# Two gate products behind the first scores of the attention phase, and both halves of a split weight taken into its plan

## The chip, the cores and the metric

The kernel runs on one core of one Trainium2 chip. The metric is the device time of one execution in microseconds; of several executions the median is taken. The core has five engines with instruction queues of their own: TensorE (PE in the profile, matrix products into PSUM), VectorE (DVE), ScalarE (ACT), GpSimd (POOL) and SyncE (SP, here for DMAs alone). An engine runs its queue in order and waits for others on semaphores.

## What is computed

One layer over 1024 tokens of width 1024 with 256 context tokens, in float32. Two attentions run side by side on one projection of the modulated input: A sees a window of 128 tokens to each side plus the context, B sees everything. Both are merged with sigmoid gates per channel, go through an output product, a residual and a layer norm, and then a feed-forward part with a short convolution. What the change touches is this part:

```python
proj = h @ w_in + b_in
o_a = _windowed_attention(q_a, k_a, v_a, k_a_c, v_a_c, sink.reshape(A_KV_HEADS, A_GROUPS))
o_b = _global_attention(q_b, jnp.concatenate([k_b, k_b_c], axis=1), jnp.concatenate([v_b, v_b_c], axis=1))
g_a, g_b = jnp.split(jax.nn.sigmoid(gate_logits), 2, axis=-1)
return (g_a * (o_a @ w_branch_a) + g_b * (o_b @ w_branch_b)) @ w_out
```

## The kernel before

Matrix products are made in three passes, since each float32 operand is split into a rounded high part and the rest as a low part: high x high, high x low, low x high (`mm3`, lines 345 to 347). Whoever makes such a pair casts the value (line 337 in `split`, or 1145) and subtracts the cast from it (342, or 1151). Much of the work of ACT, VectorE and POOL is this splitting.

The run has three phases. In the first, to 333.5 us, the input is modulated and projected. The steps stand in a fixed order (`GORD`), in which the 16 gate blocks of 128 channels fill in between the other projections; the last four stand at the end. `gate(f, hf)` makes one half of a block: 24 matmuls of 512 columns into a PSUM bank, a Sigmoid on ACT (line 920), and a store to the DRAM tensor `sgd`, issued from ACT's queue (921). Blocks 0 to 7 are A's gates, 8 to 15 are B's.

The second phase, 333.5 to 734 us, is the attention. It has 32 units: branch (16 units of A, then 16 of B), block i of 128 tokens, and key head g with its four query heads. A unit goes through these steps:

- scores of four heads on TensorE (`s` or `pt` banks, lines 720 and 721, with a mask, 743 or 745);
- per head the maximum and its negative on VectorE (`pm`, line 754), then the exponential on ACT (`ex`, line 763), which also sums. For A the sink logit stands in an extra column of the probabilities `pa`, which POOL writes once (line 1029);
- the reciprocal of the sums (782), which takes a way of its own over a transpose `pts` and DMAs;
- per tile of 128 keys four transposes on TensorE (808) into a `pt` bank, whose result is cast to a high part `hi` (ACT, 1145) and a low part `lo` (VectorE, 1151; for a few tiles POOL), and then two matmuls with V into the bank `av` (817);
- a copy of `av` by ACT (1165), then on POOL the steps `up`, `ot` (822), the multiplication by the reciprocal (1176), and the high and low part of the output tile `O` (834 and 831);
- two units ahead, the query is split, transposed (699), cast (704) and moved by DMAs (708, 709).

The order of this phase on all five engines is written by a list planner. `graph` makes one entry per step, with a cost of its engine from the table `COST`, a due time from the table `KEY`, what it follows and which buffers it takes (`RINGS`; the PSUM banks are three `pt`, two `s` of two banks, one `av`). `plan` then picks, engine by engine, the entry that is due first among those that can start within `SLACK` of the earliest, out of the next `LOOK`. The kernel is recorded in that order, so none of the constants acts at run time.

Into the plan go also the output product of A, and a part of B's. That product with `w_b` has eight channel blocks f, each in two token halves hf; a weight block holds two values of f. `group` (12 matmuls, 2.7 us) makes one half of one f, and VectorE multiplies by the gate (`gmul`, line 1064). Weight block 0 of B is split by POOL within the plan (hwb1_0, lwb1_0), and the first halves of f = 8 and 9 (the 0 and 1 of B) are made there. Blocks 1 and 2 are loaded at the end of the plan. After it, ACT casts and VectorE subtracts them, TensorE makes the first halves of f = 2 and 3 with block 1 (`half`), then the second halves of 0 and 1 (`rest`), which need the output of the last unit, and so on up to 7. `merge` adds A's and B's part and splits the sum. Then follow the product with `w_out` and the third phase, which the change leaves alone.

Of the kernel before, what the change touches and what calls it, by code (L numbers as in the profile page):

```python
# [13 lines left out]
P = 128  # L14
D = 1024
T = 1024
# [26 lines left out]
POOLED, FILL, SUMS = ((3,), (2, 6)), (16.57, 27.12), ('ot1', 'ot1')  # L43
LOOK, SLACK = 16, (0, 0, 0, 0.038, 0)
# [25 lines left out]
class Buf:  # L70
    def __init__(self, ring, slot=None):
        self.ring, self.fix, self.slot, self.left, self.end = ring, slot, None, 0, 0.0
# [13 lines left out]
def plan(ops, rings, free, look, slack):  # L86
# [5 lines left out]
    while any(todo):  # L92
# [25 lines left out]
        for b in o.uses:  # L118
# [20 lines left out]
    bm=(DVE, .61, .77), sd=(SP, .6, 9.0), sp=(POOL, 1.2, 10.0),  # L139
)  # L140
PORT = "nr1", "ot0", "ot1", "qlo", "pl", "tt", "ol", "wl"

RINGS = dict(pt=3, s=2, av=1, qs=1, q1=2, q2=2, p=8, hi=4, lo=4, ptr=2, up=1, ot=1, rb=2, wraw=1, wh=1, wl=1)

KEY = {'qh': -2.357, 'qt': -0.903, 'sc': 0.037, 'scs': (0.114, 0.286),
           'scx': -0.84, 'tr': 0.706, 'tru': (0.168, 0.1),
           'av': 1.325, 'st': 1.084, 'out': 1.875, 'exd': 0.896, 'st1': 1.52, 'wb': 29.511, 'wg': 32.061}
# [3 lines left out]
def graph(x, key=KEY, pooled=((3,), (2, 6)), fill=None, ot=("ot0", "ot1")):  # L151
# [12 lines left out]
    avs_of = {}  # L164
    units = []
    for u in range(UNITS):
# [36 lines left out]
        for h in range(4):  # L203
# [6 lines left out]
            o = op(f"sc{br}", k, lambda u=u, h=h, s=s: x.sc(u, h, s), [qr], [s], [q1, q2])  # L210
            if nar:
                o.occ, o.lat = o.occ - .11, o.lat - .11
            chain("sc", o)
            m = op(f"pm{br}", k, lambda u=u, h=h, s=s, p=p[h]: x.pm(u, h, s, p), [o, other[h] if br else None],
                   [p[h]], [s])
            chain("pm", m)
            e = op(f"ex{br}", k + key["exd"], lambda u=u, h=h: x.ex(u, h), [m], uses=[p[h]])
# [79 lines left out]
    raw = Buf("wraw")  # L297
    k = key["wb"]
    a = op("ld", k, lambda r=raw: x.ld(4, r), [units[27]["qlo"], grps[-1]], [raw])
    b_ = op("wh", k + .1, lambda r=raw: x.wh(4, r, None), [a], uses=[raw])  # L300
    c = op("wl", k + .1, lambda r=raw: x.wl(4, r, None), [b_], uses=[raw])
    for n in (0, 1):
        pt = Buf("pt")
        d = op("sg", UNITS - 1 + .1 * n, lambda f=8 + n: x.sg(f, 0), end)
        e = op("grp", key["wg"] + .3 * n, lambda f=8 + n, p=pt: x.grp(f, 0, p), [b_, c] + [units[u]["ol"] for u in range(16, 24)], [pt])
        op("bm", UNITS - .5 + .1 * n, lambda f=8 + n, p=pt: x.bm(f, 0, p), [e, d], uses=[pt])
        op("ld", UNITS - .8 + .1 * n, lambda f=1 + n: x.rw(f), end)
# [15 lines left out]
def layer_kernel(  # L323
# [348 lines left out]
    class Unit:  # L672
# [57 lines left out]
        def scores(self, h, s):  # L730
            kh = self.br * 2 + self.g
            if h == 0 and not self.br:
                self.begin()
# [1399 lines left out]
```

## Time and profile before

| | us |
|---|---|
| median of three runs | 1532.3 (1531.63 to 1532.4) |
| the profiled execution | 1530.37 |
| its span, first to last instruction | 1528.6 |
| TensorE busy | 1512.9 |
| VectorE, ACT, POOL busy | 1144.8, 802.1, 773.5 |

The profiled execution lies 1.9 us below the median, and 1.8 us of it lie around the span. The clock that TensorE was granted is full throughout. In the rows of the profile, a name left of `<-` is the tile that is written, those right of it are read; a bracket at the end gives the idle time of the engine just before the instruction and what released it. A matmul's duration is modelled and reaches over the start of the next one, so that the distance between starts tells more of TensorE's pace than the durations do.

### The profile page before, as it was taken

Reading aid. Unit: us, or ns where it says so; the run is one execution under the profiler, and the core shown is the slowest. Engines: PE = TensorE matmul, PEld = TensorE weight load, DVE = VectorE, ACT = ScalarE, POOL = GpSimd, SP = SyncE. Lnnn points to the kernel's source line nnn. Section 1 sums busy time; section 2 is a strip of 40 time slices with the busy share of each in tenths; the row PEclk is TensorE's granted clock in tenths of the full one; section 3 lists DMA queues with packets and bytes.
Section 4 is the critical chain, followed back from the end, with each engine's and each line's share of the span. In section 5 each row is a group of like instructions: output and inputs, shape, how many; then the busy total and the mean of one; then the engine's idle time right before and its main releaser. Section 6 shows DMA issues by size and latency. Waiting matters only on the chain. (4 is left out here: it accounts for less than half of the span.)

```text
span 1528.6 us, 21924 instructions
## 1 busy us (share of the span) xinstructions
PE 1512.9 (99%) x7652; PEld 1269.9 (83%) x7652; DVE 1144.8 (75%) x1719; ACT 802.1 (52%) x1404; POOL 773.5 (51%) x737
## 2 busy tenths in 40 slices
PE   9999999999999999999999999999999999999997
PEld 7888888888988888888788988888888888888886
DVE  7488847627776777787665878888888887656797
ACT  5422223449887777798332574444444444435543
POOL 0365303418887565574333556666676674021063
PEclk9999999999999999999999999999999999999999
DMA  9667663312256663742460222333334446996723
GB/s 379 236 234 254 213 239 110 100 49 56 57 151 157 176 149 79 169 95 68 169 173 35 97 86 108 112 110 112 112 102 111 110 111 177 373 281 207 253 91 111
DMA packets 111873, 229.73 MB, mean 150 GB/s; under 512 B 13489, under 2 KB 27313, under 8 KB 111666
## 3 DMA queue, kind: packets, MB, share of 16 engines
q1 hardware_dynamic: 96464, 199.20, 39.0%
q0 software_dynamic: 10400, 20.19, 8.4%
q10 hardware_dynamic: 4898, 8.94, 1.6%
q8 instruction: 60, 0.98, 0.3%
q14 instruction: 51, 0.42, 0.1%
HBM read 177.09 MB, written 65.87 MB: 159 GB/s over the span
## 5 line engine op out<-in xcount | busy, mean ns | idle before, releaser
L1151 DVE TENSOR_TENSOR lo<-pt,hi 128x512 fp32r<-128x512 f32 x188 | 126.4, 688 | 42.8 <-ACT hi L1145 41.3
L342 DVE TENSOR_TENSOR ld<-rd,hd 128x1024 fp32r<-128x1024 f32 x77 | 97.8, 1287 | 49.6 <-ACT hd L337 47.4
L1145 ACT CAST hi<-pt 128x512 fp32r<-128x512 f32 x188 | 109.6, 584 | 47.3 <-PE pt L808 39.1
L337 ACT CAST hd<-rd 128x1024 fp32r<-128x1024 f32 x77 | 79.4, 1050 | 85.8 <-PE p L347 55.7
L345 PE MATMUL p<-hd 128*128 128x512 f32 x264 | 103.2, 391 | 0.0
L346 PE MATMUL p<-ld,hd 128*128 128x512 f32 x264 | 102.8, 389 | 0.2 <-DVE ld L342 0.2
L347 PE MATMUL p<-hd,ld 128*128 128x512 f32 x264 | 102.8, 389 | 0.0
L817 PE MATMUL av<-lo,VT 128*128 128x512 f32 x236 | 101.5, 435 | 0.2 <-POOL lo L1151 0.2
L817 PE MATMUL av<-hi,VT 128*128 128x512 f32 x236 | 100.5, 433 | 0.0
L347 PE MATMUL g<-hh,wlg 128*128 128x512 f32 x256 | 99.7, 390 | 0.4 <-POOL wlg L342 0.4
L345 PE MATMUL g<-hh,whg 128*128 128x512 f32 x256 | 99.9, 390 | 0.0
L346 PE MATMUL g<-hl,whg 128*128 128x512 f32 x256 | 99.6, 389 | 0.0
L754 DVE TENSOR_SCALAR_CACHE_REDUCE p<-s,cvt,nmc 128x1024 f32<-128x1024 f32 x64 | 85.8, 1340 | 16.4 <-PE s L721 9.3
L342 POOL TENSOR_TENSOR wlg<-wg,whg 128x512 fp32r<-128x512 f32 x32 | 45.3, 1423 | 99.3 <-ACT whg L337 93.7
L763 ACT ACTIVATE p<-p,nm 128x1024 f32<-128x1024 f32 x64 | 74.0, 1157 | 13.0 <-DVE p L754 12.4
L808 PE MATMUL pt<-ident,p 128*128 128x128 f32 x512 | 76.8, 272 | 0.0
L808 PEld LDWEIGHTS pt<-ident,p 128*128 128x128 f32 x512 | 62.7, 140 | 15.4 <-DVE lo L1151 0.2
L337 ACT CAST wS<-s 128x512 fp32r<-128x512 f32 x76 | 45.3, 620 | 52.1 <-POOL s L1465 51.3
L720 PE MATMUL s<-KL,q 128*128 128x512 f32 (+2 forms) x184 | 72.4, 393 | 0.0
L721 PE MATMUL s<-KL,q 128*128 128x512 f32 (+2 forms) x184 | 69.0, 375 | 0.2 <-DMA q<-q 0.2
L337 ACT CAST wA<-ru 128x512 fp32r<-128x512 f32 x57 | 35.5, 623 | 59.6 <-PE d L347 31.8
L342 DVE TENSOR_TENSOR wS<-s,wS 128x512 fp32r<-128x512 f32 x57 | 55.5, 1000 | 11.1 <-ACT wS L337 11.1
(432 smaller groups left out, 5019.2 us busy)
## 6 DMA issues: line engine op xcount, KB each, us to landing
wml<-in_wmodT_dram SPq DMA_DIRECT2D x48, 512.0 KB
ru<-in_w_up_dram SPq DMA_DIRECT2D x38, 512.0 KB
rd<-td SPq DMA_DIRECT2D x55, 256.0 KB
rd<-sd SPq DMA_DIRECT2D x44, 256.0 KB
rd<-in_w_dn_dram SPq DMA_DIRECT2D x33, 256.0 KB
wm<-in_wmodT_dram SPq DMA_DIRECT2D x16, 512.0 KB
wg<-in_w_g_dram SPq DMA_DIRECT2D x32, 256.0 KB
sgd<-sg ACTq DMA_DIRECT2D x32, 256.0 KB
```

What stands on the lines that cost most here:

```text
L337: cast[:] = [nc.scalar.copy(hi, src).ins]
L342: low[:] = [lo_eng.tensor_tensor(out=lo, in0=src, in1=hi.bitcast(F32), op=ALU.subtract).ins]
L345: nc.tensor.matmul(ps, a[0], b[0], start=start, stop=False, skip_group_check=resumed)
L346: nc.tensor.matmul(ps, a[0], b[1], start=False, stop=False, skip_group_check=resumed)
L347: return nc.tensor.matmul(ps, a[1], b[0], start=False, stop=stop, skip_group_check=resumed).ins
L720: nc.tensor.matmul(o, self.q1[:, hs], ks, start=True, stop=False)
L754: nc.vector.tensor_scalar(out=p if self.br else p[:, self.pad + 1:SINK + 1], in0=self.sv[h], scalar1=self.scale()[:, hs] if self.br else - ...
L763: nc.scalar.activation(o, i, AF.Exp, bias=self.nm[:, hs], scale=-1.0, accum_out=acc)
L808: nc.tensor.transpose(tr[:, h * P:(h + 1) * P], src, ident)
L817: nc.tensor.matmul(self.av, v, self.parts[n][low], start=first, stop=self.left == 0)
L1145: nc.scalar.copy(hi, units[u].parts[n])
L1151: e.tensor_tensor(out=lo, in0=src, in1=hi.bitcast(F32), op=ALU.subtract)
```

## The change

It has three parts.

1. The two halves of gate block 15 are left out of the projection loop. Behind it come first the scores of unit 0, all four heads, into the banks of `pt0`, `pt1`, `s0` and `s1`; then the 48 matmuls of gate 15 into the banks of `pt2` and `av0`; then the plan. The sigmoid of this block is made as 1 / (1 + exp(-x)): Exp on ACT (`ge`), plus one on POOL (`ga`), eight reciprocals of 128 x 128 on VectorE (`gr`), and two stores from SP (`gd`), all of them planned. The sink columns of `pa` are written in two portions of four, the second one planned.
2. Blocks 0 and 1 of `w_b` are both split by POOL within the plan, into spare output tiles, and the first halves of all four f = 0 to 3 are made there. Only block 2 is loaded at the end of the plan and split behind it. After the plan come the second halves of f = 0 to 3 (`rest`), each followed by its merge, then f = 4 to 7 with both halves (`both`).
3. `KEY`, `FILL`, `LOOK` and `SLACK` have new values, and narrow units count as cheaper, so that the plan orders the whole phase anew.

```diff
-POOLED, FILL, SUMS = ((3,), (2, 6)), (16.57, 27.12), ('ot1', 'ot1')
-LOOK, SLACK = 16, (0, 0, 0, 0.038, 0)
+POOLED, FILL, SUMS = ((3,), (2, 6)), (16.13, 25.4), ('ot1', 'ot1')
+LOOK, SLACK = 24, (0, 0, 0, 0.11, 0.209)
...
+    for hf in (0, 1):
+        b = Buf("pt", 2) if hf == 0 else Buf("av", 0)
+        gates.append(op("gate", -90.0 + hf, None, gates[-1:], [b]))
+        e = op("ge", key["ge"], lambda hf=hf, r=tile: x.ge(hf, r), [gates[-1]], [tile] if hf == 0 else [], [b] + [tile] * hf)
...
+        e = op("ga", key["ge"], lambda hf=hf: x.ga(hf), [e], uses=[tile])
+        for c in range(4):
+            r = op("gr", key["gr"] + .6 * (4 * hf + c), lambda hf=hf, c=c: x.gr(hf, c), [e], uses=[tile])
+        op("gd", key["gr"] + .6 * (4 * hf + c), lambda hf=hf: x.gd(hf), [r], uses=[tile])
...
+            if k == 2 * KT - 1:
+                continue
             gate(k, a)
...
+    for h, tag in enumerate(("pt0_", "pt1_", "s0_", "s1_")):
+        units[0].scores(h, ps2.tile([P, 512 * (1 + h // 2)], F32, tag=tag, name=f"s0_{h}", bufs=1))
+    gps = [ps2.tile([P, 512], F32, tag=tag, name="g15", bufs=1) for tag in ("pt2_", "av0_")]
+    for hf in (0, 1):
+        for k in range(KT):
+            w = [t[:, k % 4 * P:(k % 4 + 1) * P] for t in ready["g", 2 * KT - 1, k // 4]]
+            mm3(gps[hf], w, [t[:, hsl(hf)] for t in hT[k]], k == 0, k == KT - 1)
...
+        def ge(self, hf, r):
+            if hf == 0:
+                self.gt = at(r, "g").rearrange("p (a b) c -> p a (b c)", a=2)
+            nc.scalar.activation(self.gt[:, hf], gps[hf], AF.Exp, bias=bmc[:, 8:9], scale=-1.0)
+
+        def ga(self, hf):
+            nc.gpsimd.tensor_scalar(out=self.gt[:, hf], in0=self.gt[:, hf], scalar1=1.0, scalar2=1.0, op0=ALU.mult,
+                                    op1=ALU.add)
+
+        def gr(self, hf, c):
+            t = self.gt[:, hf, c * P:(c + 1) * P]
+            nc.vector.reciprocal(t, t)
+
+        def gd(self, hf):
+            nc.sync.dma_start(sgd[2 * KT - 1][:, hf * HALF:(hf + 1) * HALF], self.gt[:, hf])
...
-            t = ht("hwb1_0", (P, 8, P), R32) if br else at(h, f"{f2}", R32)
+            t = spare(f"hwb{f}") if br else at(h, f"{f2}", R32)
...
-    for f2 in (1, 2):
-        wb[f2] = [wq.tile([P, 8, P], R32, tag="w", name=f"{a}wb{f2}", bufs=4) for a in "hl"]
-        split(rwb[f2], *wb[f2], nc.scalar, nc.vector)
...
+    wb = {2: [wq.tile([P, 8, P], R32, tag="w", name=f"{a}wb2", bufs=4) for a in "hl"]}
+    split(rwb[2], *wb[2], nc.scalar, nc.vector)
+    hput("rwb2")
...
-    half(2, 0)
-    with tc.issue_after(half(3, 0)):
-        for f in (0, 1):
+    for f in range(KT):
+        if f < 4:
             rest(f, sml)
...
+        else:
+            both(f)
         merge(f)
         if f == 3:
             wb[3] = weight(w_b[3], "wb3", 8, he=nc.scalar, le=nc.vector, rtag=None)
```

The change adds some 30 lines to the code and shifts the lines behind them: the passes of a product stand in 374 to 376 after it, the scores in 752 and 753, the maximum in 786, the transposes in 840, the products with V in 849, the low parts in 1224.

**TensorE at the beginning of the phase.** Before, the last matmuls of gate 15 are followed by the scores of unit 0 (`pt_0_0_0` is the bank for branch 0, block 0, key head 0, head 0; numbers at the end tell buffers apart), and scores go on for all of unit 1 as well before the first transpose:

```order
L345 MATMUL g_1_2989<-hh_477,whg_1_2901 128x512
L346 MATMUL g_1_2989<-hl_478,whg_1_2901 128x512
L347 MATMUL g_1_2989<-hh_477,wlg_1_2902 128x512
L720 MATMUL pt_0_0_0_3050<-KL_2113,q_0_0_2424 128x256
L721 MATMUL pt_0_0_0_3050<-KL_2113,q_0_0_2426 128x256
L745 MATMUL pt_0_0_0_3050<-maskr,identr 128x128
L720 MATMUL pt_0_0_0_3050<-KC,q_0_0_2424 128x256
L721 MATMUL pt_0_0_0_3050<-KC,q_0_0_2426 128x256
```

After the change, the last matmuls of gate 15 are followed by the first transposes of unit 0 and then by the first scores of unit 1:

```order
L374 MATMUL g_2994<-hh_477,whg_1_2901 128x512
L375 MATMUL g_2994<-hl_478,whg_1_2901 128x512
L376 MATMUL g_2994<-hh_477,wlg_1_2902 128x512
L840 MATMUL pt_0_0_0_3083<-ident,pa_3055 128x128
L840 MATMUL pt_0_0_0_3083<-ident,pa_3056 128x128
L840 MATMUL pt_0_0_0_3083<-ident,pa_3057 128x128
L840 MATMUL pt_0_0_0_3083<-ident,pa_3058 128x128
L752 MATMUL pt_0_1_0_3093<-KL_2114,q_0_1_2482 128x256
L753 MATMUL pt_0_1_0_3093<-KL_2114,q_0_1_2484 128x256
L775 MATMUL pt_0_1_0_3093<-maskr,identr 128x128
L752 MATMUL pt_0_1_0_3093<-KC,q_0_1_2482 128x256
L753 MATMUL pt_0_1_0_3093<-KC,q_0_1_2484 128x256
```

The four scores of unit 0 now stand ahead of gate 15, and those of unit 1 between the first transposes.

**VectorE at the same place.** Before, the maxima of units 0 and 1 stand together ahead of the first low parts (`pa` are the probabilities, `sm` the sums):

```order
L754 TENSOR_SCALAR pa_3034,nm_0_1_3091<-pt_0_1_0_3090,negsink 128x512
L754 TENSOR_SCALAR pa_3035,nm_0_1_3091<-pt_0_1_1_3101,negsink 128x512
L782 RECIPROCAL sm_0_0_3052<-sm_0_0_3052 128x4
L754 TENSOR_SCALAR pa_3036,nm_0_1_3091<-s_0_1_2_3112,negsink 128x512
L754 TENSOR_SCALAR pa_3037,nm_0_1_3091<-s_0_1_3_3120,negsink 128x512
L1151 TENSOR_TENSOR lo_0_0_0_3164<-pt_0_0_0_3127,hi_0_0_0_3141 128x512
L1151 TENSOR_TENSOR lo_0_0_1_3174<-pt_0_0_1_3136,hi_0_0_1_3154 128x512
```

After the change, the first of the gate's reciprocals (`wrawg` is the tile of the gate) stands ahead of the maximum of unit 1's second head:

```order
L814 RECIPROCAL sm_0_0_3070<-sm_0_0_3070 128x4
L786 TENSOR_SCALAR pa_3059,nm_0_1_3107<-pt_0_1_0_3093,negsink 128x512
L1224 TENSOR_TENSOR lo_0_0_0_3114<-pt_0_0_0_3083,hi_0_0_0_3099 128x512
L1224 TENSOR_TENSOR lo_0_0_1_3123<-pt_0_0_1_3102,hi_0_0_1_3112 128x512
L1132 RECIPROCAL wrawg<-wrawg 128x128
L786 TENSOR_SCALAR pa_3060,nm_0_1_3107<-pt_0_1_1_3127,negsink 128x512
L1224 TENSOR_TENSOR lo_0_0_8_3158<-pt_0_0_8_3138,hi_0_0_8_3153 128x512
```

The low parts of unit 0 have moved between the maxima of unit 1, and the other seven reciprocals follow one every few rows, the last of them some fifty rows behind the maximum of unit 1's first head.

**VectorE at the end of the phase.** Before, the low splits of blocks 1 and 2 (`lwb`) stand behind the last low part of the attention, then one of `w_out` (`lwo`), and that of block 3 nowhere near:

```order
L1151 TENSOR_TENSOR lo_7_1_9_8544<-pt_7_1_9_8531,hi_7_1_9_8540 128x512
L342 TENSOR_TENSOR lwb_8576<-rwb_8387,hwb_8575 128x1024
L342 TENSOR_TENSOR lwb_8580<-rwb_8390,hwb_8579 128x1024
L342 TENSOR_TENSOR lwo_8764<-rwo_8761,hwo_8763 128x1024
L1064 TENSOR_TENSOR bT_0_8360<-b_0_1_8614,bT_0_8360 128x512
L1298 TENSOR_TENSOR bT_0_4919<-bT_0_4919,bT_0_8360 128x1024
L1064 TENSOR_TENSOR bT_1_8366<-b_1_1_8629,bT_1_8366 128x512
```

After the change, one block (2, `lwb_8626`) is split there, and the split of block 3 (`lwb_8712`) stands ahead of the merge of f = 0 (`bT_0_4884`) and of the multiplication by the gate of f = 1 (`bT_1_8391` from `b_1_1`):

```order
L1224 TENSOR_TENSOR lo_7_1_9_8579<-pt_7_1_9_8554,hi_7_1_9_8563 128x512
L1115 TENSOR_TENSOR bT_3_8412<-ptb_0_8566,bT_3_8412 128x512
L1115 TENSOR_TENSOR bT_1_8391<-ptb_0_8585,bT_1_8391 128x512
L371 TENSOR_TENSOR lwb_8626<-rwb_8414,hwb_8625 128x1024
L1115 TENSOR_TENSOR bT_0_8385<-b_0_1_8630,bT_0_8385 128x512
L371 TENSOR_TENSOR lwb_8712<-rwb_8709,hwb_8711 128x1024
L1367 TENSOR_TENSOR bT_0_4884<-bT_0_4884,bT_0_8385 128x1024
L1115 TENSOR_TENSOR bT_1_8391<-b_1_1_8650,bT_1_8391 128x512
```

One split has left this place, and the split of block 3 has come into it. On TensorE, the second halves use two PSUM buffers in turn (`sml`), so that the one of f = 3 waits for the multiplication of f = 1. On SP, the load of block 3 (`rwb_8709`) keeps its place behind the last unit's sums, but its semaphores now include POOL's low part of the last unit's output, since the tile reuses memory that is read there; before, they were those of the last product with V and of POOL's last `lo`.

More of the change, by code (lines that the diff above doesn't have):

```diff
@@ L314, in graph @@
                 put[0] = a
+    for o in ops:
+        if o.eng == PE and o.fn:
+            o.after.append(gates[1])
+    sinks.after.append(gates[1])
     return ops, units, grps
@@ L752, in most @@
             hs = slice(h, h + 1)
+            if h == 0 and not self.br:
+                self.begin()
             self.p[h] = p[:, self.pad:]
@@ L1038, in at, with sinks @@
     def at(b, name, dt=F32):
[L1039 removed]
+        pool = ps2 if b.ring in PRING else att
         return pool.tile(SHAPE[b.ring], dt, tag=f"{b.ring}{b.slot}_", name=f"{b.ring}{name}", bufs=1)
+    pa = {}
+    for n in (7, 0, 1, 2, 3, 4, 5, 6):
+        pa[n] = pp.tile([P, T], F32, tag=f"p{n}_", name=f"pa{n}", bufs=1)
+    def sinks(*ns):
+        for n in ns:
+            nc.gpsimd.tensor_scalar(out=pa[n][:, SINK + 1:SINK + 2], in0=negsink[:, n:n + 1], scalar1=1.0, scalar2=0.0,
+                                    op0=ALU.mult, op1=ALU.add)
+    sinks(0, 1, 2, 3)
     bT, wab, bacc = {}, {}, {}
```

124 lines of the change are left out of this document (65 added, 59 removed).

## Prediction

> **What bounds the kernel now.** I read the page first, then the busy time by stretches, then TensorE's own rows where a stretch is not full.
>
> ```profile
> span 1528.6 us, 21924 instructions
> PE 1512.9 (99%) x7652; PEld 1269.9 (83%) x7652; DVE 1144.8 (75%) x1719; ACT 802.1 (52%) x1404; POOL 773.5 (51%) x737
> 333.00:356.00 23.00, 21.91 (x155) 19.49 (x154) 16.95 (x41) 20.52 (x48) 11.42 (x23) 1.00 0.23 58
> 356.00:722.00 366.00, 366.00 (x2269) 313.32 (x2268) 279.73 (x589) 296.61 (x657) 255.47 (x337) 1.00 0.48 119
> 722.00:760.00 38.00, 35.33 (x172) 28.50 (x171) 21.93 (x23) 14.02 (x21) 15.88 (x20) 1.00 0.44 156
> ```
>
> TensorE sets the end: it is busy for 1512.9 of 1528.6 us, and nothing off it matters unless TensorE waits for it. The change removes no matmul and adds none, so the whole effect is in what TensorE waits for. The last three rows (after the time: busy time of PE, of the weight loads, of DVE, ACT and POOL, then the granted clock) show where that can be. The attention phase starts with 1.09 us of idle, its middle, 366 us, shows none, and the stretch around its end has 2.67 us. The clock is 1.00 in all three. Those two ends are what the change rebuilds.
>
> The listed idle understates a wait, because the ends of matmuls are modelled and overlap the next start. So I count from start to start. These are TensorE's rows at the beginning (start, duration):
>
> ```profile
> 333.02 0.39 PE L346 MATMUL g<-hl,whg 128*128 128x512 f32 x1
> 333.25 0.40 PE L347 MATMUL g<-hh,wlg 128*128 128x512 f32 x1
> 333.48 0.28 PE L720 MATMUL pt<-KL,q 128*128 128x256 f32 x1
> ...
> 338.67 0.44 PE L808 MATMUL pt<-ident,pa 128*128 128x128 f32 x2
> 339.38 0.33 PE L808 MATMUL pt<-ident,pa 128*128 128x128 f32 x1 [0.28 <-ACT pa L763]
> 340.09 0.33 PE L808 MATMUL pt<-ident,pa 128*128 128x128 f32 x1 [0.38 <-ACT pa L763]
> ...
> 340.94 0.44 PE L720 MATMUL s<-KL,q 128*128 128x384 f32 x1
> 341.63 0.42 PE L721 MATMUL s<-KL,q 128*128 128x384 f32 x1 [0.24 <-DMA q<-q]
> ...
> 355.65 0.50 PE L817 MATMUL av<-lo,VT 128*128 128x512 f32 x1 [0.19 <-POOL lo L1151]
> ...
> 371.37 0.60 PE L808 MATMUL pt<-ident,pa 128*128 128x128 f32 x4
> 371.73 0.48 PE L817 MATMUL av<-hi,VT 128*128 128x512 f32 x1
> 372.04 0.34 PE L720 MATMUL s<-KL,q 128*128 128x384 f32 x1
> 372.22 0.34 PE L721 MATMUL s<-KL,q 128*128 128x384 f32 x1
> ```
>
> A 512-column matmul that waits for nothing starts 0.23 us after the one before (333.02 to 333.25). Four free transposes take 0.36 (371.37 to 371.73), so one takes 0.09, and a 384-column score takes 0.18 (372.04 to 372.22). The first transposes of unit 0 wait for its exponentials: 338.67 to 339.38 is 0.71 for two, 0.53 too long, and 339.38 to 340.09 is 0.62 too long. The score at 341.63 comes 0.51 late. That is 1.66 us in three waits; with the small one at 355.65 I put the start at **1.9 us**.
>
> The reason is the chain behind the last gate product:
>
> ```profile
> 334.38 0.75 DVE L754 TENSOR_SCALAR_CACHE_REDUCE pa<-pt,negsink 128x512 f32<-128x512 f32 x1 [27.10 <-PE pt L721]
> 336.40 1.23 POOL L1029 TENSOR_SCALAR pa<-negsink 128x1 f32<-128x1 f32 x8
> 336.62 0.73 ACT L763 ACTIVATE pa<-pa,nm 128x513 f32<-128x513 f32 x1 [0.73 <-POOL pa L1029]
> ```
>
> The first scores start at 333.48, their maximum is taken at 334.38 for 0.75 us, and the first exponential starts only at 336.62. TensorE runs out of scores at 338.67, and the transpose that needs the fourth exponential starts at 340.09, 6.6 us after the first score.
>
> At the end of the phase (last product with V, then the output product):
>
> ```profile
> 733.76 0.45 PE L817 MATMUL av<-lo,VT 128*128 128x512 f32 x1
> 735.88 0.50 PE L345 MATMUL b<-O,hwb 128*128 128x512 f32 x1 [1.67 <-ACT hwb L337]
> 736.22 0.40 PE L346 MATMUL b<-O,hwb 128*128 128x512 f32 x1
> 737.61 0.50 PE L347 MATMUL b<-O,lwb 128*128 128x512 f32 x1 [1.00 <-DVE lwb L342]
> ```
>
> From 733.76 to 735.88 is 1.89 us more than a matmul takes, from 736.22 to 737.61 is 1.16 more: **3.05 us** of waiting for the split of the weight block that ACT and VectorE make after the plan.
>
> **The change at the start.** The 48 matmuls of gate 15 move behind the scores of unit 0: 48 x 0.23 = 11 us on TensorE, more than the 6.6 us that unit 0's maxima and exponentials need. The three waits above go. What is late next: only unit 0 was scored ahead; before, units 0 and 1 were. So unit 1's scores, maxima and exponentials now run between unit 0's transposes and products. Walking the new order of all engines with the durations above and these (groups of instructions between 333 and 470 us: count, busy us, mean ns),
>
> ```profile
> L1151 DVE TENSOR_TENSOR lo<-pt,hi 128x512 fp32r<-128x512 f32 x62 | 42.3, 689 | 15.4 <-ACT hi L1145 14.4 <-POOL qs L694 0.5 <-POOL hi L1140 0.2
> L754 DVE TENSOR_SCALAR_CACHE_REDUCE pa<-s,negsink 128x640 f32<-128x640 f32 x48 | 42.0, 881 | 8.1 <-PE s L721 7.2 <-PE pt L808 0.7
> L782 DVE RECIPROCAL sm<-sm 128x4 f32<-128x4 f32 x17 | 3.0, 174 | 2.1 <-ACT pa L763 1.7
> L781 DVE TENSOR_TENSOR sm<-sm,smc 128x4 f32<-128x4 f32 x1 | 0.2, 158 | 0.0
> ```
>
> I find five short waits in the first 13 us after the first transpose: 0.1 for unit 0's first high part, which stands behind the second gate exponential on ACT; 0.3 for the maximum of unit 1's first head, whose bank the next query transpose needs (0.9 after its scores start, then 0.75); 0.4 for unit 1's fourth exponential (the four run between casts); 0.4 and 0.1 for a maximum and a low part that stand behind one of the new reciprocals. That is **1.3 us**. The removed sigmoids and their two stores were in ACT's idle time and give nothing.
>
> The eight new reciprocals of 128x128 on VectorE are in no row. Between four columns, a reciprocal costs 0.174 and an addition 0.158, so 4 ns more per column; the subtraction of 512 columns costs 0.689, about 1 ns per column. I estimate 0.158 + 128 x 5 ns = 0.8 us each, 6.4 us in all. The floor is 0.17, the cost of the 4-column row; the far end, 32 times that row, is 5.6 each, which its fixed part makes too much; I keep 0.2 to 1.5. They stand among the first 53 VectorE operations of the phase, which cover some 37 us. VectorE is 74% busy in the first stretch and 76% in the middle, so those 37 us have about 9 free. Eight at 0.8 fit, but raise it to 93%, and each delays the maximum or low part behind it; I add 0.3 us. Start after: 1.6 against 1.9, **-0.3** (-1.9 if all of it is covered, +2.4 if the reciprocals cost 1.5: 12 us into 9 free leaves 3 over, less what the first 13 us had counted).
>
> [...]
>
> The "+1" on POOL and the two stores on SP are beside: POOL had 11.6 us idle in the first stretch. SP issues the first store only after four reciprocals, with the sums of unit 3 and the rotated queries of unit 6 behind it; both are needed more than a unit later.
>
> **The middle.** The new constants reorder the whole phase, but 366.00 of 366.00 us are busy, so little is to be had. The high and low parts of branch B now mostly stand further ahead of the products that use them in TensorE's order. Since half of a short wait hides in modelled ends (the 1.66 us above are listed as 0.90), I allow **-0.7**, between -2 and +1. The second weight block's split goes to POOL, which has 110 us idle here.
>
> **The end.** Both waits of 3.05 us go, for blocks 0 and 1 are split in the plan. TensorE goes on with one group of 12 and six matmuls of the next, then needs the last unit's output in its high and low part. What makes that, in the old run (the last two rows are groups between 333 and 740 us):
>
> ```profile
> 735.86 3.37 DVE L342 TENSOR_TENSOR lwb<-rwb,hwb 128x1024 fp32r<-128x1024 f32 x2 [2.21 <-ACT hwb L337]
> 735.74 2.40 POOL L822 TENSOR_TENSOR ot<-ptra,up 64x256 f32<-64x256 f32 x2
> 738.23 1.60 POOL L1176 TENSOR_TENSOR ot<-ot,rb 128x256 f32<-128x256 f32 x1
> 740.40 0.73 POOL L831 TENSOR_TENSOR O<-ot,O 128x256 fp32r<-128x256 f32 x1
> L822 POOL TENSOR_TENSOR ot<-ptra,up 64x256 f32<-64x256 f32 x64 | 47.7, 745 | 3.5
> L1176 POOL TENSOR_TENSOR ot<-ot,rb 128x256 f32<-128x256 f32 x32 | 24.4, 764 | 0.9
> ```
>
> It was done at 741.13, 7.37 us after the last product with V. Beside the two subtractions, POOL's steps took 2.40 and 1.60 where their means are 1.49 and 0.76: 1.75 us of contention. One subtraction of the two is left. Without contention the low part is there at 5.6; I take 5.9, bounds 5.6 and 7.4. TensorE reaches the matmul that needs it after 20 starts, 4.5 us. **New wait 1.4** (1.1 to 2.9).
>
> [...]
>
> Then comes a wait that the old order did not have. The output product of f = 3 in the second half needs a bank from f = 1, whose multiplication stands on VectorE behind the low split of block 3 (moved up from behind the merge of f = 3) and one merge. Block 3's load, issued at about 734.3 before, now waits for memory that the last unit's low part frees. How long such a load takes, from the w_out block that was issued at that place:
>
> ```profile
> 741.53 0.43 SPq L1259 DMA_DIRECT2D rwo<-in_w_out_dram  x1
> 745.97 1.05 ACT L337 CAST hwo<-rwo 128x1024 fp32r<-128x1024 f32 x1 [9.19 <-DMA rwo<-in_w_out_dram]
> 747.05 1.23 DVE L342 TENSOR_TENSOR lwo<-rwo,hwo 128x1024 fp32r<-128x1024 f32 x1 [7.82 <-ACT hwo L337]
> 748.19 0.68 DVE L1064 TENSOR_TENSOR bT<-b,bT 128x512 f32<-128x512 f32 x1
> 748.91 1.50 DVE L1298 TENSOR_TENSOR bT<-bT,bT 128x1024 f32<-128x1024 f32 x1
> ```
>
> Counted from the low part: issue 0.4, landing 4.44, cast 1.08, subtraction 1.14, merge 1.3, multiplication 0.7: 9.1 us. TensorE has 29 matmuls until then, 6.6 us. **New wait 2.5**; nothing if the load lands within 1.9 us, 3.5 if it takes a microsecond more. The end is 1.4 + 2.5 - 3.05 = **+0.8** (-2.0 to +3.3). Behind it the order is the old one; the later 0.5 us for the first w_out blocks stays.
>
> **The sum** is -0.3 - 0.7 + 0.8 = -0.2 on the profiled execution of 1530.37 us (span 1528.6 and 1.8 around it). The median of the runs is 1532.3, 1.9 above it; against that I forecast **1532.1 us**.
>
> **Rivals.** *Everything late is covered* (0.20): the load lands before its bank is asked for and POOL runs free, so the end is 1.1 - 3.05 = -2.0; the start keeps 0.9 of its 1.9 and the middle gives 1.5: -4.5, 1527.8 us. For it: all named waits of before go. Against: 4.44 us of landing in the row. *VectorE fills up* (0.19): from 1.15 us for a reciprocal, the eight take all 9 us that VectorE has free in the first 37 us, and each further 0.1 costs 0.8. At 1.4 the start is 2.0 longer; with the end at +1.5 and nothing from the middle, +3.5: 1535.8 us. For it: no row shows the operation, the order puts it ahead of maxima. Against: my 0.8. *The gate only moves the wait* (0.12): the cover that gate 15 gives to unit 0 is what unit 1 loses, the start stays 1.9, the middle stays, and the end gives +0.8: 1533.1 us. That the gate might wait itself I leave out: the last sigmoid before it frees the third score bank during the first two heads' 1.2 us.
>
> **How the numbers follow.** The forecast has 0.49, and its own range is 1530 to 1534.5. The range of **1528.2 to 1536.0** takes in most of both outer rivals. About 0.2%, 3.1 us, is what a measurement of this kernel can tell from no change: faster than 1529.2 is 0.20, the first rival; slower than 1535.4 is 0.18, most of the second; same 0.62.
>
> **What would show it.** Right: no wait of TensorE for unit 0's exponentials; short ones for maxima near the new reciprocals; after the last product with V a wait on POOL's output of about 1.4 and one on VectorE's multiplication of about 2.5 before f = 3. Wrong: reciprocals over 1.2 us, a load of block 3 that lands within 2 us, or idle time in the middle of over 1 us.

## The result and the profile after

The changed kernel takes 1542.08 us (median of five runs, 1540.56 to 1542.46) against 1531.83 (five runs, 1531.63 to 1532.4): the ratio is 1.0064, with a 95% interval of 1.0049 to 1.0079. It is slower by 10 us, where 1532.1 was forecast, and it lies outside the range. The profiled execution took 1540.56 us. The head of the page of the changed kernel:

```profile
span 1538.8 us, 21952 instructions
```

The waits of TensorE in the changed kernel, longest first (us in total, times, longest; rows between left out):

```profile
PE a L374 <- DVE c L1691: 6.3, 1, 6.3
PE b L374 <- POOL O L866: 1.2, 1, 1.2
...
PE b L374 <- DVE bT L1115: 0.9, 1, 0.9
```

The second and the third are those that the prediction named at the end of the attention. The first is one that it knew nothing of. It stands in the third phase, some 170 us behind the last product whose order was changed. TensorE's rows there, after:

```profile
940.64 0.39 PE L376 MATMUL u<-B,lwu 128*128 128x512 f32 x1
947.33 0.76 PE L374 MATMUL a<-B,wA 128*128 128x512 f32 x1 [6.30 <-DVE c L1691]
947.89 0.63 PE L375 MATMUL a<-B,wA 128*128 128x512 f32 x1
948.32 0.63 PE L376 MATMUL a<-B,wA 128*128 128x512 f32 x1
...
950.88 0.53 PE L376 MATMUL a<-B,wA 128*128 128x512 f32 x1
951.24 0.39 PE L374 MATMUL a<-B,wA 128*128 128x512 f32 x1
951.47 0.40 PE L375 MATMUL a<-B,wA 128*128 128x512 f32 x1
```

And the same place of the kernel before, with the convolution's last step on VectorE:

```profile
938.25 0.39 PE L347 MATMUL u<-B,lwu 128*128 128x512 f32 x1
938.47 0.39 PE L345 MATMUL a<-B,wA 128*128 128x512 f32 x1
943.59 1.27 DVE L1633 SCALAR_TENSOR_TENSOR c<-u,cvt,c 128x1023 f32<-128x1023 f32 x1
```

Before, the first matmul of `a` follows the last of `u` after 0.22 us, although the convolution's last step on VectorE (L1633; L1691 in the changed kernel) begins only 5 us later; after, it starts 6.69 us behind `u`, when that step is done. Then nine matmuls start 0.43 us apart on average in place of 0.23: from 947.33 to 951.24 is 3.91 us for nine, 1.9 more than 9 x 0.227. So the place costs 6.5 + 1.9 = **8.3 us**. The windows show the second part as the granted clock (the number before the DMA share); the first three rows are the stretches that the prediction was built on:

```profile
333.00:356.00 23.00, 22.32 (x153) 20.05 (x152) 17.10 (x38) 18.31 (x42) 14.31 (x24) 1.00 0.20 47
356.00:722.00 366.00, 364.62 (x2247) 310.55 (x2246) 281.60 (x588) 294.19 (x651) 260.36 (x337) 1.00 0.50 122
722.00:760.00 38.00, 35.38 (x173) 28.32 (x172) 20.09 (x26) 13.94 (x23) 14.19 (x18) 1.00 0.36 127
...
940.00:945.00 5.00, 1.03 (x5) 0.52 (x3) 5.00 (x5) 3.35 (x5) 3.29 (x2) 0.93 0.00 0
945.00:950.00 5.00, 2.67 (x6) 2.15 (x7) 4.93 (x5) 0.00 (x0) 1.87 (x2) 0.50 0.79 262
950.00:955.00 5.00, 5.00 (x21) 4.09 (x20) 1.42 (x3) 1.25 (x3) 3.81 (x3) 0.89 0.44 161
```

The clock is 0.50 in the stretch in which TensorE starts again and 0.89 in the next.

What `a` waits for stands on VectorE, in the changed kernel:

```profile
944.12 1.27 DVE L1689 SCALAR_TENSOR_TENSOR c<-u,cvt,c 128x1023 f32<-128x1023 f32 x1
945.31 0.68 DVE L371 TENSOR_TENSOR wA<-ru,wA 128x512 fp32r<-128x512 f32 x1
945.91 1.27 DVE L1691 SCALAR_TENSOR_TENSOR c<-u,cvt,c 128x1023 f32<-128x1023 f32 x1
```

The last of these reads the tile u1_2 out of PSUM, and `a` (the first tile of this part, a3) is about to be written into the same bank. Neither TensorE's order nor VectorE's differs there from before; the banks do. The pool `ps3` holds a ring of three tiles of two banks (`big`) and one of two tiles of one bank (`sml`), and lays them out in the order in which each is first asked for. Before, the first product behind the plan was `half(2, 0)`, which takes a `big` tile: `big` got banks 0 to 5, `sml` 6 and 7, and u1_2 lay in 0 and 1. After, `rest(0)` comes first and takes an `sml` tile: `sml` gets banks 0 and 1, `big` 2 to 7, and u1_2 lies in 6 and 7. The next pool hands out its banks by a list written by hand, `PSU = 6, 7, 2, ...`, so a3 goes to bank 6 in both kernels: free before, u1_2's after. The part ahead of the prediction says that the change leaves the third phase alone; that holds for its order, not for its banks.

The end of the attention phase in the changed kernel, first TensorE's rows with waits:

```profile
745.26 0.49 PE L374 MATMUL b<-O,hwb 128*128 128x512 f32 x1 [1.15 <-POOL O L866]
746.07 0.50 PE L375 MATMUL b<-O,hwb 128*128 128x512 f32 x1 [0.32 <-POOL O L863]
...
753.93 0.50 PE L374 MATMUL b<-O,hwb 128*128 128x512 f32 x1 [0.95 <-DVE bT L1115]
```

POOL's last two steps, the high and the low part of the last output tile:

```profile
743.95 1.26 POOL L866 TENSOR_SCALAR O<-ot 128x256 fp32r<-128x256 f32 x1
745.29 0.73 POOL L863 TENSOR_TENSOR O<-ot,O 128x256 fp32r<-128x256 f32 x1
```

The issue of block 3's load on SP's queue:

```profile
746.04 0.33 SPq L1331 DMA_DIRECT2D rwb<-in_w_b_dram  x1
```

Its cast on ACT:

```profile
749.83 1.05 ACT L366 CAST hwb<-rwb 128x1024 fp32r<-128x1024 f32 x1 [8.22 <-DMA rwb<-in_w_b_dram]
```

And VectorE, from the split of block 2 to the multiplication of f = 1:

```profile
743.39 1.55 DVE L371 TENSOR_TENSOR lwb<-rwb,hwb 128x1024 fp32r<-128x1024 f32 x1
...
750.91 1.23 DVE L371 TENSOR_TENSOR lwb<-rwb,hwb 128x1024 fp32r<-128x1024 f32 x1 [2.67 <-ACT hwb L366]
752.05 1.22 DVE L1367 TENSOR_TENSOR bT<-bT,bT 128x1024 f32<-128x1024 f32 x1
753.19 0.69 DVE L1115 TENSOR_TENSOR bT<-b,bT 128x512 f32<-128x512 f32 x1
```

Block 3 is loaded only from 746.04, when the low part of the last unit (745.29, 0.73 long) is written, and its chain load, cast, split, merge, multiplication ends at 753.88, just ahead of the matmul at 753.93.

To see where else time went, I summed over TensorE's rows how much each start comes later than the median distance in the kernel before for the same pair of shapes. This is "lost" in the table below, in us. The zero of a column depends on the stretch from which the medians are taken, so only differences within a column are to be read. Most kernels of the next section are in it, each in one profiled execution. Such an execution can lie off its median, by 2.5 us in the last row (1535.16 against 1532.63). Two further kernels that run as B does up to 700 us lose 0.6 less than B in the first column and 1.3 more in the second: so much can differ between executions there.

| kernel | ratio to before | 320-356 | 356-460 | 460-730 | 730-760 | 760-1000 |
|---|---|---|---|---|---|---|
| before | 1 | 3.5 | 6.6 | 16.9 | 3.2 | -3.7 |
| after | 1.0064 | 2.5 | 9.8 | 17.4 | 3.2 | 4.0 |
| before, banks renumbered | 1.0058 | 3.4 | 6.6 | 17.2 | 3.1 | 4.2 |
| after, banks renumbered (B) | 1.0008 | 2.4 | 9.7 | 17.2 | 3.2 | -3.9 |
| B, block 3 in other memory | 0.9998 | 3.0 | 9.7 | 17.2 | 1.9 | -4.5 |
| B, old plan constants | 1.0009 | 2.3 | 7.9 | 18.2 | 6.4 | -4.5 |
| B, old constants, block 3 in other memory | 0.9975 | 2.3 | 8.0 | 18.2 | -0.3 | -4.5 |
| weights alone | 0.9973 | 3.4 | 6.6 | 18.1 | 0.1 | -4.5 |
| weights alone, block 3 over the last output | 1.0005 | 3.4 | 6.7 | 18.0 | 5.9 | -4.5 |

### The profile page after: what moved, and what is told of

It is laid out like the page before. It is cut to its first block, busy times and chain, and to the rows that moved or that the text cites. A ratio compares the mean times of both kernels' runs of the same rounds, so it can differ in the third digit from the quotient of the medians.

```text
span 1538.8 us, 21952 instructions
## 1 busy us (share of the span) xinstructions
PE 1516.7 (99%) x7652; PEld 1271.8 (83%) x7652; DVE 1142.5 (74%) x1729; ACT 803.6 (52%) x1403; POOL 780.6 (51%) x741
## 4 chain that ended last, share of the span: by engine, by line
PE 90%; DVE 4%; POOL 2%; issue 2%; ACT 1%; DMA 1%; DVEq 0%; SPq 0%; POOLq 0%; ACTq 0%
PE av L849 7%; PE pt L840 6%; PE g L376 4%; PE g L374 4%; PE g L375 4%; PE p L374 4%; PE p L376 4%; PE p L375 4%; PE s L752 3%; PE s L753 3%; PE a L374 2%; PE a L375 2%; PE a L376 2%; PE d L375 2%; PE c L375 2%; PE d L376 2%
## 5 line engine op out<-in xcount | busy, mean ns | idle before, releaser
L786 DVE TENSOR_SCALAR_CACHE_REDUCE pa<-s,negsink 128x640 f32<-128x640 f32 (+1 forms) x58 | 49.2, 856 | 24.0 <-PE s L753 19.3
```

Source lines behind the costliest of these rows:

```text
L786: nc.vector.tensor_scalar(out=p if self.br else p[:, self.pad + 1:SINK + 1], in0=self.sv[h], scalar1=self.scale()[:, hs] if self.br else - ...
```

## The experiments

My first theory was that the banks cost 8.3 of the 10 us; its rival that the third phase is late for another reason, such as VectorE, which stands 2.3 us later there. Two mirrored runs decide it. The order of all engines stays in both.

**The changed kernel with renumbered banks.**

```diff
-PSU = 6, 7, 2, 3, 4, 5, 0, 1
-PSO = 4, 5, 0, 1, 7, 6, 2, 3
+PSU = 0, 1, 2, 3, 4, 5, 6, 7
+PSO = 4, 5, 6, 7, 1, 0, 2, 3
```

> The changed kernel with the two lists of PSUM banks of the feed-forward phase renumbered (0 with 6, 1 with 7), nothing else. Theory of the bank: the 6.3 us of idle that the changed kernel shows before the product a of the first three-product tile (listed as waiting for the convolution's last step on VectorE) is there because that tile takes the very bank which the convolution still reads; with the old pairing of banks the wait goes, and with it the stretch of lower clock behind it (0.50 and 0.89): 8.3 us less, about 1533.7 us. Rival, theory of lateness: VectorE comes to that step later than before because the phases ahead of it are longer; then the wait stays, within 1 us of 1542.

Measured: 1532.8 us, ratio 1.0008 (0.9999 to 1.0017); TensorE has no wait at `a`. Against 1.0064 that is 0.56%, some 8.6 us.

**The kernel before with the same renumbering.**

> The kernel before with its two lists of PSUM banks renumbered in the same way (0 with 6, 1 with 7), nothing else; the order of all engines stays. Theory of the bank: the first three-product tile now takes the bank that the convolution reads, so the kernel before gets the same wait of 6.3 us and the lower clock behind it, 8.3 us more, about 1540.1 us, at the same place. Rival, lateness: the kernel before is on time there, so within 1 us of 1531.8.

Measured: 1540.64 us, ratio 1.0058 (1.0045 to 1.007). The first of TensorE's waits in it:

```profile
PE a L345 <- DVE c L1633: 6.3, 1, 6.3
```

It is the same wait to the tenth, in a kernel that has no other line changed. So the bank list and the layout cost what was measured, and the rival falls.

**The layout put right in place of the list.** The first `rest` takes a `big` tile, so that `big` is laid out first again; the list stays as it was.

```diff
-            rest(f, sml)
+            rest(f, sml if f else lambda n: big(n)[:, 0:HALF])
```

> The change with its own bank list, but the first second half (f = 0) takes a buffer of the large ring in place of the small one, so that the large ring is laid out first, in banks 0 to 5, as before the change. If the order of first allocation is what did it, the first three-product tile a3 (bank 6) waits for nothing. But the large ring is now one step on, and the last up product u1_2 lies in banks 2 and 3, those of the third three-product tile c3, 24 matmuls later: 24 x 0.227 = 5.4 us of the 6.3 are covered, so I expect a wait of 0.9 us at c3 on the same VectorE instruction, no drop of the granted clock, and 1532.8 + 0.9 = 1533.7 us (1533.2 to 1534.2). Rival: the bank list itself or something else in the feed-forward phase is slow; then the 6.3 us stay, at 1541 to 1543 us.

Measured: 1534.54 us, ratio 1.002 (1.0011 to 1.0028), 0.12% over the renumbered banks or 1.8 us, where 0.9 was expected. The wait at `a` is gone, and TensorE has the one that was worked out for the third tile:

```profile
948.21 0.47 PE L374 MATMUL c<-T13h,wS 128*128 128x512 f32 x1 [0.91 <-DVE c L1691]
```

The window around it (the clock is the number before the DMA share):

```profile
945.00:950.00 5.00, 4.09 (x19) 3.08 (x18) 4.93 (x6) 0.20 (x1) 0.96 (x1) 1.00 0.67 213
```

The wait is 0.91 as foretold, on the same VectorE instruction, and the clock stays at 1.00. So the order of first allocation is shown too. The other 0.9 us lie within what the intervals leave open.

With the banks mended, the change is at 1.0008: no gain. Four runs ask where the rest is.

**The low part of block 3 on POOL**, on top of the renumbered banks.

```diff
-            wb[3] = weight(w_b[3], "wb3", 8, he=nc.scalar, le=nc.vector, rtag=None)
+            wb[3] = weight(w_b[3], "wb3", 8, he=nc.scalar, le=nc.gpsimd, rtag=None)
```

> As the first run of this set, and the low part of weight block 3 of the output product is subtracted by POOL in place of VectorE. If the 1.1 us before the second half of f = 3 is VectorE standing at the split of block 3 (whose load lands late) with the gate's multiplication behind it, that wait goes and the time falls by 1.1 us against the first run. If the multiplication is late for another reason, within 0.3 us of it; if POOL is too slow for block 3 (about 2.4 us in place of 1.2), a new wait before f = 6 shows.

Measured: 1532.13 us, ratio 1.0001 (0.9993 to 1.001). TensorE's wait on VectorE before f = 3 is gone; the median is 0.7 us lower, which the intervals do not separate from nothing.

**The reciprocals over 4 columns in place of 128**, on the renumbered banks. This leaves most of the division of gate 15 out.

```diff
-            t = self.gt[:, hf, c * P:(c + 1) * P]
+            t = self.gt[:, hf, c * P:c * P + 4]
```

> As the first run of this set, and each of the eight reciprocals of the gate runs over 4 columns in place of 128 (the rest of that gate block keeps the value one plus exponential; this leaves most of the division out). VectorE's order is the same, with 6.2 us less work in the first 37 us of the attention. If these reciprocals cause the 3.1 us by which TensorE's starts between 356 and 460 us fell behind the kernel before, most of it comes back: 2 to 3 us less than the first run. If the new order of the plan causes it (query transposes and low parts on POOL), the time is within 0.5 us of the first run.

Measured: 1532.49 us, ratio 1.0006 (0.9997 to 1.0014), 0.3 us below the renumbered banks. The loss from 356 to 460 us is 9.7 with them as without. The reciprocals are not what costs there.

**The old constants of the plan**, on the renumbered banks: `KEY` but for its new entries, `FILL`, `LOOK`, `SLACK` and the costs of narrow units as before.

```diff
-LOOK, SLACK = 24, (0, 0, 0, 0.11, 0.209)
+LOOK, SLACK = 16, (0, 0, 0, 0.038, 0)
...
-           'av': 1.292, 'st': 1.191, 'out': 1.297, 'exd': 0.565, 'st1': 1.248, 'wb': (28.06, 28.638),
+           'av': 1.325, 'st': 1.084, 'out': 1.875, 'exd': 0.896, 'st1': 1.52, 'wb': (28.06, 28.638),
```

> The change with the renumbered banks, and with the plan constants of before (KEY apart from the new entries, FILL, LOOK 16, SLACK, no cheaper narrow units). It keeps the gate behind the first scores and both weight blocks in the plan. With the banks alone the kernel took 1532.8, and it lost 9.7 us between 356 and 460 us of the span where before lost 6.6. My theory: the reordering by the new constants makes those 3 us. Then this stretch falls back to about 6.6, the start keeps its gain of 1.0, the end stays, and the time is 1530 us (1529.3 to 1531). Rival: the moved gate makes them, since only one unit is scored ahead and every query transpose and low part of branch A comes nearer to the product that needs it; then the stretch stays at 9 to 10 and the time at 1532 to 1533.

Measured: 1533.02 us, ratio 1.0009 (1.0 to 1.0017). The time is the rival's, the reason is neither's. The stretch from 400 to 460 us does fall from 7.1 to 4.3, as the theory said, but 356 to 400 rises from 2.6 to 3.6, and the end from 3.2 to 6.4.

**The weights alone**: the kernel before with the second part of the change and renumbered banks; gate 15 and the constants as before.

```diff
-           'av': 1.325, 'st': 1.084, 'out': 1.875, 'exd': 0.896, 'st1': 1.52, 'wb': 29.511, 'wg': 32.061}
+           'av': 1.325, 'st': 1.084, 'out': 1.875, 'exd': 0.896, 'st1': 1.52, 'wb': (28.06, 28.638), 'wg': (31.993, 33.356, 33.022, 33.265)}
...
-            t = ht("hwb1_0", (P, 8, P), R32) if br else at(h, f"{f2}", R32)
+            t = spare(f"hwb{f}") if br else at(h, f"{f2}", R32)
...
-    half(2, 0)
-    with tc.issue_after(half(3, 0)):
-        for f in (0, 1):
+    for f in range(KT):
+        if f < 4:
             rest(f, sml)
+        else:
+            both(f)
```

> The kernel before with the second part of the change alone: both weight blocks split by POOL in the plan, second halves and merges behind it, gate 15 and the constants as before; banks renumbered as in the run of the banks. The stretch from 356 to 460 us then stays at 6.6 and the start at 3.5, in either theory. At the end: the two waits for the split of the weight block (3.05 us) go and come back as one on POOL's output part (1.9 as in the trace of after) and one on the merge's multiplication (1.1), so the sum is nil: 1531.6 us (1530.8 to 1532.3). Rival: the extra 3.5 us of POOL splitting in the plan delay branch B's last units, 1533 us or more, with idle time of TensorE between 640 and 734.

Measured: 1527.66 us, ratio **0.9973** (0.9962 to 0.9984): faster than both kernels, by 4 us, which neither theory had. TensorE loses 0.1 us from 730 to 760; the one wait of its rows that is left there:

```profile
749.32 0.50 PE L346 MATMUL b<-O,hwb 128*128 128x512 f32 x1 [0.20 <-DVE bT L1065]
```

SP's issue of block 3's load in this kernel:

```profile
730.30 0.33 SPq L1263 DMA_DIRECT2D rwb<-in_w_b_dram  x1
```

The load is issued at 730.30, ahead of the last product with V, and not behind the last output part. Its tile has the same address in both kernels. What lay there earlier is what differs: in this kernel probabilities of branch B, last read by the transposes of the last unit; in the changed kernel the tiles `ot` and `up` of the last unit. For the first part of the change took the probabilities and the sums out of the pool `att` into a pool `pp` of its own, and that moved everything else in `att`. The front part of this text says that the load's semaphores changed, and not which part of the change did it.

**The old constants, with the low part of block 3 on POOL** (both edits above).

> The run with the plan constants of before, and in addition the low part of weight block 3 on POOL in place of VectorE. In the kernel with the new constants this took 0.7 us. My theory: the same here, 1529.4 us if the old constants give 1530, which would be faster than before by 0.14%. Rival: with the output part earlier or later the wait it removes isn't there, and it is equal to the run without it.

Measured: 1534.15 us, ratio 1.0024 (1.0015 to 1.0034). Neither: it is slower. In it TensorE has one long wait at the end in place of two:

```profile
754.70 0.80 PE L370 MATMUL b<-O,hwb 128*128 128x512 f32 x1 [5.54 <-DVE bT L1111]
```

POOL's split of block 3, ahead of it:

```profile
746.08 2.39 POOL L367 TENSOR_TENSOR lwb<-rwb,hwb 128x1024 fp32r<-128x1024 f32 x1 [4.93 <-ACT hwb L362]
```

POOL takes 2.39 us for what VectorE does in 1.23, and the load comes as late as ever. The nine executions of this kernel spread from 1533.44 to 1539.86 us, and the profiled one, 1537.07, is above the median. What is left is where the load waits, which the next three runs test.

**Block 3's load over other memory**, on the renumbered banks. Its slot and that of the first `w_out` block are exchanged; the addresses are fixed beforehand, since this pool too is laid out in the order of first use.

```diff
+            for pool, tag in hfree[0:8]:
+                pool.tile([P, T], F32, tag=tag, name="lay" + tag, bufs=1)
+            hfree[0], hfree[7] = hfree[7], hfree[0]
             wb[3] = weight(w_b[3], "wb3", 8, he=nc.scalar, le=nc.vector, rtag=None)
```

> The run of the renumbered banks (1532.8), and the load of weight block 3 now trades its place in SBUF with the first w_out block: its 4 KB lie over probabilities of branch B that are read for the last time two units before the end, no longer over the tiles ot and up of the last unit. Order and work are the same. My theory: the load is then issued at about 728 us in place of 744.8, and the wait of 1.1 us on VectorE before f = 3 goes; the wait of 1.9 on POOL's output part stays: 1531.7 us (1531.2 to 1532.2). Rival: POOL's split or VectorE's order makes that wait, not the load's memory, and it stays at 1532.8.

Measured: 1531.08 us, just below the expected range, ratio 0.9998 (0.9989 to 1.0007). The ratio is 0.10% below that of the banks alone, which the intervals do not separate from nothing; the trace shows what went. SP issues the load 15 us earlier than in the run of the banks alone:

```profile
729.51 0.58 SPq L1331 DMA_DIRECT2D rwb<-in_w_b_dram  x1
```

Of TensorE's two waits the one on VectorE is gone, the one on POOL is left:

```profile
744.85 0.50 PE L374 MATMUL b<-O,hwb 128*128 128x512 f32 x1 [1.14 <-POOL O L866]
745.66 0.50 PE L375 MATMUL b<-O,hwb 128*128 128x512 f32 x1 [0.31 <-POOL O L863]
```

**The same exchange with the old constants.**

> The run of the gate with the plan constants of before (1533.0, where the stretch from 734 to 760 us lost 6.3 us in two waits of 2.2 and 2.6 and in matmuls at a lower clock behind them), with the same trade of memory for block 3. My theory: block 3's load was issued at 741.4 behind the last output part, against 730.3 in the run of the weights alone, which lost nothing there. With the memory traded the 6.3 us go: 1526.9 us (1526 to 1528), faster than before by 0.3%. Rival: the moved gate itself costs, elsewhere than at the end; then no more than 1.1 us come back, 1532.

Measured: 1528.12 us, ratio **0.9975** (0.9966 to 0.9985), against 1.0009 without the exchange: 5.2 us, where 6.3 were expected. TensorE has no listed wait from 733 to 760 us. This is the whole change, apart from its constants, with both layouts mended, and it is as fast as the weights alone.

**The opposite: the same exchange in the run of the weights alone**, where the other slot lies over `up` and `ot` of the last unit.

> The opposite: the run of the weights alone (1527.7), with the same trade of slots, which in its layout puts block 3 over ot and up of the last unit. My theory: the load is issued 11 us later, behind the last output part, and the waits and the lower clock of the gate run with the old constants come back: 1527.7 + 6.3 = 1534.0 us (1532 to 1535). Rival: nothing of the kind, 1527.7.

Measured: 1532.63 us, ratio 1.0005 (0.9996 to 1.0014): 0.32%, 4.9 us slower than without it, where 6.3 were expected. SP's issue of the load:

```profile
741.41 0.33 SPq L1263 DMA_DIRECT2D rwb<-in_w_b_dram  x1
```

TensorE's waits:

```profile
748.03 0.50 PE L346 MATMUL b<-O,hwb 128*128 128x512 f32 x1 [1.81 <-DVE bT L1065]
...
753.77 0.78 PE L346 MATMUL b<-O,hwb 128*128 128x512 f32 x1 [2.27 <-DVE bT L1065]
```

And the window behind the second of them:

```profile
755.00:760.00 5.00, 5.00 (x18) 4.01 (x18) 4.87 (x5) 2.11 (x2) 1.06 (x1) 0.78 0.50 173
```

The load comes 11.1 us later, and with it two waits of 4.1 us and a granted clock of 0.78. The exchange moves the time in opposite directions in the two kernels, so it is the memory under the load that decides.

## Why the prediction was wrong

**The step that failed** is one sentence at the end of the part on the end: "Behind it the order is the old one; the later 0.5 us for the first w_out blocks stays." The first half is true, and it was taken to mean that the waits are the old ones too. An instruction waits for what its order says and for whoever used its buffer last: `a` waited 6.30 us for the reader of its bank, in an order that had not changed. TensorE's order behind the phase was compared; the banks and the semaphores of the same rows were not. They held the 8.3 us (0.56% in the runs), more than all terms of the sum together. The second half is wrong in the other direction: the 0.5 us listed for `w_out` went, some 0.7 by starts.

The rest of the difference was in the sum, but not as the sum had it:

- **The start: -0.3 predicted, -1.0 measured** (3.5 to 2.5 in the table). The two waits for unit 0's exponentials went, as said; the third, of a score for its query's DMA, is there again for another unit (0.48 listed at 355.64). Of the five short waits that were to come in their place one is listed, on the maximum of unit 1's first head, 0.21.
- **The reciprocals: 0.8 us each estimated, 0.947 measured:**

```profile
L1132 DVE RECIPROCAL wrawg<-wrawg 128x128 f32<-128x128 f32 x8 | 7.6, 947 | 0.0
```

That is 0.15 above the estimate, 1.2 us for all eight. The rival that needed more than 1.15 did not come. With 4 columns the median is 0.3 us lower, which the intervals do not separate from nothing.

- **The middle: -0.7 predicted, with at most +1; about +3.7 measured** (6.6 to 9.8 and 16.9 to 17.4). It is the term that was most off after the banks, and I had given 366 us of a full TensorE as the reason that little is to be had. That holds for a gain, not for a loss. The first two of the few waits listed for TensorE from 400 to 460 us in the changed kernel:

```profile
427.80 0.50 PE L849 MATMUL av<-lo,VT 128*128 128x512 f32 x1 [0.18 <-POOL lo L1224]
428.49 0.54 PE L731 MATMUL pt<-identr,qs 128*128 128x128 f32 x4 [0.19 <-POOL qs L726]
```

They come to 0.8 by starts; most of the loss of 7.0 is in steps that are each too short to be listed. With the old constants this stretch goes back to 4.3, so the new constants make it. The two runs with block 3 in other memory, with the new and with the old constants, differ by 0.23% in the ratios and 3.0 us in the medians: that is the price of the new constants once block 3 is not late. By the table most of it lies elsewhere than in the middle: 2.2 at the end, 0.7 at the start, and in the middle 1.7 less 1.0. The end is the wait on POOL's output. With the old constants two groups of first halves, 24 matmuls, stand between the last product with V and the second halves (from 734.59 in the run with block 3 in other memory), with the new ones a single group of 12 (from 739.87 in the changed kernel), so that 2.7 us less of TensorE's work covers POOL's last steps. The gate by itself moves its loss: in the run with the old constants and block 3 in other memory the start loses 1.1 less than in the run of the weights alone, 356 to 460 us 1.4 more, and the two have the same time. So the third rival, that the gate only moves the wait, was right for that part.

- **The wait on POOL's output: 1.4 predicted, 1.9 measured** (743.72 to 745.26 and 745.26 to 746.07, less 0.23 each). The low part was there 6.4 us after the last product with V, not 5.9. The cast of the output stood beside VectorE's split of block 2 (743.39, 1.55 long) and took 1.26 us, against 0.41 for the same cast in the other units. That is 0.85 more. I had allowed 0.3 for it, where POOL's steps beside two such splits had taken 1.75 us more before.
- **The wait for block 3: 2.5 predicted, 1.1 measured.** The load was to be on its way for 4.44 us; from the issue at 746.04 to the cast at 749.83 are 3.79, 0.65 less. The 0.4 for the issue were counted twice, since the 4.44 begin at the issue; it followed the low part after 0.02. The steps behind the load took 0.2 less than the 4.2 reckoned, and TensorE took 0.2 more for its 29 matmuls: 2.5 - 0.65 - 0.4 - 0.2 - 0.2 = 1.05. The sum of the end, +0.8 predicted, comes to 0 (3.2 and 3.2 in the table).
- **What was not seen there** is that this wait was no part of the second change. Without the first part, the load is issued 11 us before the last output part is written, and the same work at the end loses nothing: 0.9973. The prediction had named the cause, memory that the last unit's low part frees, and had then only asked how long the load takes, not which edit had put it over that memory.

Added up from the ratios, one after the other: banks +0.56%, block 3's memory +0.10%, new constants +0.23%, and what is left of the change -0.25%. The two in the middle depend on their order: with block 3 left where it was, the constants make no difference (1.0008 and 1.0009), and under the old constants block 3's memory is worth 0.34%.

## What to carry to other kernels

An identical order of instructions is not an identical program: compare what each row waits for and where its tile lies, to the end of the kernel, for a hand-written list of banks is right only for one layout of the pool ahead of it. Pools that lay out in the order of first use turn the moving of a product or the splitting of a pool into a change of every address behind it. If a change that removes waits gains nothing, try its parts alone with the layout held still: here one of three parts was worth 0.27%, and two layouts and a table of constants gave more than that back.

## What the runs showed of the hardware

Some waits of TensorE came with a lower granted clock and so cost more than their length. After 6.30 us of idle in the changed kernel the next nine matmuls started 0.43 us apart in place of 0.23 (1.9 us more). In windows of half a microsecond the granted clock there was 1.00 up to 944.0, 0.82 in the next, 0.50 from 944.5 to 951.0, 0.85 in the next and 1.00 from 951.5: it fell within the wait, which began behind the matmul of 940.64, and was full again between 3.7 and 4.2 us after the restart at 947.33. In the run of the weights with block 3 over the last output, 2.27 us of idle, 3.5 us behind another 1.81, gave a window with 0.78 of the clock. A single 0.91 us, in the run with `big` laid out first, left its window at 1.00, and so did 1.67 and 1.00, a few matmuls apart, before the change. Why 1.81 and 2.27 lowered the clock where 1.67 and 1.00 did not, these runs do not show.
